# Two compression products and two heads of second attention in column halves, zero products and two DMA queues at the start

## The chip, the cores and the metric

The kernel runs on one core of one Trainium2 chip. The metric is device time in microseconds (us) of one execution, from the first instruction to the last. Engines are named as in the profile: PE (TensorE matmul), PEld (its weight loads), DVE (VectorE), ACT (ScalarE), POOL (GpSimd), SP (SyncE, which issues nearly all DMAs here).

## The reference, cut to what matters

The program is a decoder trunk of two layers over 256 tokens of width 1024, in float32. Each sub-layer is `x <- LayerNorm(alpha * x + sublayer(x))`.

- Layer 0: sliding-window attention (16 query heads, 4 key and value heads of 64), then a dense SwiGLU of inner width 3584.
- Layer 1: sparse attention (compressed, selected and window branches, each with its gate), then 8 SwiGLU experts, two for each token.

The change touches the compressed keys and values, and the last product of attention:

```
def compress(t, pos, w1, w2):
    blk = t[:, idx] + pos[None, None, :, None, :]
    flat = blk.transpose(0, 1, 3, 2, 4).reshape(B, nc, Hkv, CMP_LEN * HEAD_DIM)
    return jax.nn.gelu(flat @ w1) @ w2
kcc = compress(kc, pos_k, ck_w1, ck_w2)
vcc = compress(vc, pos_v, cv_w1, cv_w2)
...
o_s = jnp.einsum('bkgqs,bkqsd->bqkgd', p_s.astype(vsel.dtype), vsel)
```

There are 15 blocks for each of 4 key heads, laid out as 64 rows; `flat` has 2048 columns and the hidden width is 256.

## The kernel before, in words

**Tiles.** The 256 tokens are two tiles of 128 (t = 0, 1). Weights come from HBM in pieces of 1 MB into buffers called `raw` (7 of them), in the order that `plan` wrote; `load` issues them on SP as buffers come free. For the dense layers each piece is split into `hi` on ACT (L120) and `lo` on DVE (L121), in three buffers of each, and a product takes three matmuls (L204 to L206). The weights of the compression (four pieces, `w1s`) and of the experts are not split and are used as float32. Later the experts' weights also use buffers `more` and `later`, which exist once the attention's memory is given back.

**The start.** SP issues a part of the constants `cf`, both halves of the first token tile `x0`, the first two weight pieces (two DMAs each), the second token tile, and two more pieces. PE transposes x0 (L224), ACT and DVE split that into `Th` and `Tl`, and PE multiplies the first two pieces with token tile 0, then transposes x1 and does the same for tile 1. PE's order is written out by hand there; the order on ACT and DVE is a list scheduler's.

**Compression** (`compress`, L778). `X` holds keys (k = 0) and values (k = 1), laid out so that 64 of its columns are the stationary operand. For k, for each of two weight pieces q, eight matmuls of 64 columns by 256 (L803) accumulate into `hc[:, k, :]`, on PSUM partitions 0 to 63. Between k = 0 and k = 1, PE does the 16 transposes of the selected keys (`kd`, L391). A GELU follows on `hx`, 64 partitions by 512 (L807 to L815), then four transposes (L820), and two small products into `kcc` and `vcc`.

**Second attention** (`unit`, L905). For each of 8 head pairs j there are three units: (t=1, head 0), (t=1, head 1) and (t=0, both heads). A unit is a generator of four steps: scores and exponentials; division; transposes of the probabilities into `pt`; products of `pt` with values (L948) into `po`. The product of head h goes to partitions 64h to 64h + 63 of `po`. A unit of t = 1 does its four products in a row, all in one half; the unit of t = 0 alternates the halves. `attention` starts a unit each round and runs the steps of older units, the last one LAG + 1 = 4 rounds later. Tiles `p` and `pt` share eight buffers with the tag "pt".

**Experts.** For each expert, gate and up products (L1187, L1195), then down products (L1210, L1216), with weights streamed by SP.

Of the kernel before, what the change touches and what calls it, by code (L numbers as in the profile page):

```python
# [9 lines left out]
F32 = mybir.dt.float32  # L10
F32R = mybir.dt.float32r
BF16 = mybir.dt.bfloat16
# [6 lines left out]
P = 128  # L19
# [4 lines left out]
HD = 64  # L24
# [11 lines left out]
CMP_HID = 256  # L36
# [48 lines left out]
def trunk(ctx: ExitStack, tc: tile.TileContext, a, out, dbg=None):  # L85
    nc = tc.nc
    dbg = dbg or {}
    PE, ACT, DVE, POOL, SP = nc.tensor, nc.scalar, nc.vector, nc.gpsimd, nc.sync

    const = ctx.enter_context(tc.tile_pool(name="const", bufs=1))  # L90
# [6 lines left out]
    def bank(dtype=F32):  # L97
        return psum.tile([P, 512], dtype, name="ps", tag="ps")


    cbf = const.tile([P, 3 * P], BF16, name="cbf")
    cf = const.tile([P, 2 * P + 3 * NE + 9], F32, name="cf")
# [24 lines left out]
    order, raws, ready = [], [], []  # L127
# [17 lines left out]
    def plan(src, exact=True, pieces=1):  # L145
        kt, cols = src.shape[0] // P, src.shape[1]
        n = max(i for i in range(1, PART // cols + 1) if kt % i == 0)
        for k0 in range(0, kt, n):
            order.append((lambda k0=k0: src[k0 * P:(k0 + n) * P, :], n, cols, exact, pieces))
# [8 lines left out]
    def load():  # L158

        while state["loaded"] < len(order) and len(raws) < state["ahead"]:  # L160
            src, n, cols, exact, pieces = order[state["loaded"]]
            state["loaded"] += 1
            raw, kind = new_raw()
            raw = raw[:, :n * cols].rearrange("p (k f) -> p k f", k=n)
            src = src().rearrange("(k p) f -> p k f", p=P)
            pieces = min(n, pieces if state["loaded"] < len(order) - 2 else 2)
            for k in range(0, n, n // pieces):
                SP.dma_start(raw[:, k:k + n // pieces, :], src[:, k:k + n // pieces, :])
            raws.append((raw, exact, kind))
# [23 lines left out]
    def take(count=1, spare=None):  # L193

        spare = max(0, LIVE - count) if spare is None else spare
        while (raws or state["loaded"] < len(order)) and len(ready) < count + spare:
            feed()
        parts = ready[:count]
        del ready[:count]
        return parts  # L200
# [260 lines left out]
    wa, wo = a["a_w_in"][0], a["a_w_out"][0]  # L461
    plan(wa[:, :512], pieces=2)
    for c in (1024, 512):
# [19 lines left out]
    KC, VC, KS, VS, KW, VW, GL = (1024 + 256 * k for k in range(7))  # L483
    w1s = [a[w][0, q * 1024:(q + 1) * 1024, :] for w in ("b_cmp_k_w1", "b_cmp_v_w1") for q in range(2)]
    plan(wb[:, KC:KC + 512])
# [50 lines left out]
    with tc.tile_pool(name="swa", bufs=1) as pool:  # L536
# [52 lines left out]
        ps_kv, ps_q = {}, [{}, {}]  # L589
        with tc.manual_schedule(engines={PE.engine}):  # L590
            for _ in project(Ts, 512, ps_q[0], 2):
                pass
# [147 lines left out]

    zeros = const.tile([P, P], BF16, name="zeros")
    POOL.memset(zeros, 0.0)
    SP.dma_start(cmask, a["cmask"].rearrange("(t p) k c -> p t k c", p=P))
    with tc.tile_pool(name="nsa", bufs=1) as pool:
# [33 lines left out]
        def compress():  # L778
# [5 lines left out]
            DVE.tensor_copy(posT, pb[:, :32].rearrange("p (a b) -> p a b", a=2))  # L784
            hc = bank().rearrange("p (k h) -> p k h", k=2)[:C]
            Xs = wts.tile([P, 2, CMP_LEN // 2, NKV, CP], F32, name="X", tag="raw", bufs=RAW)
            for k in range(2):
# [10 lines left out]
                yield  # L798
            for k in range(2):
                for q in range(2):  # L800
                    (r,), = take()
                    for i in range(8):
                        PE.matmul(hc[:, k, :], Xs[:, k, q * 8 + i].rearrange("p g c -> p (g c)"), r[:, i, :],  # L803
                                  start=q == 0 and i == 0, stop=q == 1 and i == 7, skip_group_check=True)
                yield
            hx, hy = (pool.tile([P, 2, CMP_HID], F32, name="hx", tag="pt", bufs=PT)[:C] for _ in range(2))
            ACT.activation(hx, hc, AF.Copy)  # L807
# [8 lines left out]
            yield  # L816
            pb = bank().rearrange("p (k j c) -> p k j c", k=4, j=2)[:, :2, :, :]
            for k in range(2):
                for j in range(2):
                    PE.transpose(pb[:, k, j, :], hx[:, k, j * P:(j + 1) * P], ident[:C, :C])  # L820

# [80 lines left out]

        sums = {}

        def unit(t, j, heads):  # L905
# [36 lines left out]
            yield  # L942
            if heads[0] == 0:
                sums[t, j] = bank()[:, :P]
            po = sums[t, j]
            for m, (i, br, k) in enumerate(steps):
                h = heads[i]
                PE.matmul(po[h * HD:(h + 1) * HD, :], v[:, k, br, g, :], pt[:, m * P:(m + 1) * P],  # L948
                          start=k + br == 0, stop=False, skip_group_check=True)
            if heads[-1] == 1:  # L950
                PE.matmul(po, vcc[:, j // 4, j % 4].rearrange("p e d -> p (e d)"), pcT[:, t, j // 4, :], start=False,
                          stop=True, skip_group_check=True)
                split(oTs[t][0][:, j, :], oTs[t][1][:, j, :], po)
# [501 lines left out]
```

## Time and profile before

| | us |
|---|---|
| runs shown | 1411.89, 1413.41, 1418.05 |
| median | 1413.41 |
| the profiled execution, its own time | 1413.78 |
| its span in the trace | 1412.0 |
| PE busy | 1360.7 (96%) |
| DVE busy | 442.0 (31%) |
| ACT busy | 342.4 (24%) |

The stages by the trace: first attention to about 85 us, dense SwiGLU to about 345, second attention with its projections and the compression to about 505, the end of the layer and the router to about 545, the experts to the end. PE's busy time counts overlapping matmuls once and their ends are modelled, so a full slice may still hold slack; the time from the start of one group to the start of the next is what counts.

### The profile page before, as it was taken

The page shows a single profiled execution, that of the slowest core. Times are in us where ns is not written, and L with a number is a line of the kernel's source. Part 1 is how long each engine was busy: PE and PEld are TensorE (multiplying, and loading weights), DVE is VectorE, ACT ScalarE, POOL GpSimd, SP SyncE. Part 2 cuts the span into 40 slices and gives each one's busy share as a digit, 9 for nine tenths or more (in the row PEclk, how much of TensorE's full clock was granted, in tenths as well). Part 3 has the DMA queues.
Part 4 walks back from the last instruction along what each step waited for, and adds up shares of the span by engine and source line. Part 5 has one row for each costly group of instructions (what it writes and reads, how often), then busy time and mean ns, then how long its engine had stood idle before and what let it go on. Part 6 is the DMA issues. An engine that isn't in the chain of part 4 may idle for free. (4 is left out here: it accounts for less than half of the span.)

```text
span 1412.0 us, 23279 instructions
## 1 busy us (share of the span) xinstructions
PE 1360.7 (96%) x9761; PEld 784.5 (56%) x9762; DVE 442.0 (31%) x1004; ACT 342.4 (24%) x783; POOL 8.4 (1%) x17
## 2 busy tenths in 40 slices
PE   7999999999999999999999999999998999999984
PEld 6777888887777774453344354444343454445331
DVE  6876544556958753000101001100100100200103
ACT  5754444444456721010001001000101000100100
POOL 0000000000000000000000000000000000000000
PEclk9999999999999998999999999999999999999997
DMA  9516565554372067899999999999999999999994
GB/s 349 181 61 211 181 192 192 179 179 155 122 271 91 31 266 272 345 389 377 409 403 409 407 401 409 408 402 407 408 402 409 408 401 408 408 395 393 408 402 179
DMA packets 143679, 434.86 MB, mean 308 GB/s; under 512 B 11312, under 2 KB 18128, under 8 KB 143568
## 3 DMA queue, kind: packets, MB, share of 16 engines
q1 hardware_dynamic: 138416, 428.85, 79.3%
q10 hardware_dynamic: 5152, 4.45, 1.0%
q8 instruction: 79, 1.29, 0.4%
q14 instruction: 32, 0.26, 0.1%
HBM read 432.23 MB, written 1.05 MB: 307 GB/s over the span
## 5 line engine op out<-in xcount | busy, mean ns | idle before, releaser
L121 DVE TENSOR_TENSOR lo<-raw,hi 128x512 fp32r<-128x512 f32 (+2 forms) x244 | 166.4, 730 | 106.5 <-ACT hi L120 106.3
L1187 PE MATMUL ps<-more,Th 128*64 128x512 f32 (+1 forms) x920 | 186.8, 555 | 5.7 <-DMA more<-in_moe_w_gate 5.4
L120 ACT ACTIVATE hi<-raw 128x512 fp32r<-128x512 f32 (+2 forms) x244 | 146.0, 659 | 142.4 <-PE ps L206 129.5
L204 PE MATMUL ps<-hi,Th 128*128 128x512 f32 (+1 forms) x432 | 171.4, 397 | 4.4 <-ACT hi L120 3.2
L206 PE MATMUL ps<-hi,Tl 128*128 128x512 f32 (+1 forms) x432 | 168.6, 391 | 1.4 <-DVE Tl L121 1.4
L205 PE MATMUL ps<-lo,Th 128*128 128x512 f32 (+1 forms) x432 | 168.3, 390 | 0.0
L1244 DVE TENSOR_TENSOR h<-h,ps 128x512 f32<-128x512 f32 (+1 forms) x32 | 19.9, 621 | 448.4 <-PE ps L1187 448.4
L1187 PE MATMUL ps<-later,Th 128*64 128x512 f32 (+1 forms) x680 | 128.9, 525 | 2.1 <-DMA later<-in_moe_w_gate 1.8
L1187 PEld LDWEIGHTS ps<-more,Th 128*64 128x64 f32 x920 | 65.0, 138 | 115.5 <-issue 98.4
L204 PEld LDWEIGHTS ps<-hi,Th 128*128 128x128 f32 x432 | 81.9, 190 | 23.6 <-ACT hi L120 3.6
L1187 PE MATMUL ps<-raw,Th 128*64 128x512 f32 (+1 forms) x448 | 94.4, 561 | 0.6 <-ACT Th L1095 0.6
L1210 PE MATMUL ps<-more,hTa 128*64 128x512 f32 x408 | 92.2, 595 | 2.7 <-DMA more<-in_moe_w_down 2.7
L1236 ACT ACTIVATE h<-ps 128x512 f32<-128x512 f32 (+1 forms) x32 | 17.4, 544 | 315.1 <-PE ps L1187 315.1
L206 PEld LDWEIGHTS ps<-hi,Tl 128*128 128x128 f32 x432 | 81.8, 189 | 20.4 <-DVE Tl L121 2.9
L205 PEld LDWEIGHTS ps<-lo,Th 128*128 128x128 f32 x432 | 82.0, 190 | 16.8 <-DVE lo L121 0.4
L1187 PEld LDWEIGHTS ps<-later,Th 128*64 128x64 f32 x680 | 47.8, 137 | 72.1 <-issue 60.1
L1210 PE MATMUL ps<-later,hTa 128*64 128x512 f32 x312 | 70.3, 594 | 2.0 <-DMA later<-in_moe_w_down 2.0
L1210 PEld LDWEIGHTS ps<-more,hTa 128*64 128x64 f32 x408 | 28.4, 137 | 60.6 <-issue 54.6
L1187 PEld LDWEIGHTS ps<-raw,Th 128*64 128x64 f32 x448 | 31.7, 139 | 53.1 <-issue 48.6
L1195 PE MATMUL ps<-more,Th 128*32 128x256 f32 (+1 forms) x1136 | 60.2, 359 | 0.0
L1239 ACT ACTIVATE hb<-ps 128x256 f32<-128x256 f32 (+1 forms) x20 | 7.2, 358 | 189.0 <-PE ps L1195 189.0
L1243 DVE TENSOR_TENSOR hb<-hb,ps 128x256 f32<-128x256 f32 (+1 forms) x20 | 7.8, 388 | 142.3 <-PE ps L1195 142.3
(256 smaller groups left out, 1444.5 us busy)
## 6 DMA issues: line engine op xcount, KB each, us to landing
more<-in_moe_w_up SPq DMA_DIRECT2D x53, 1024.0 KB, 18.1
more<-in_moe_w_down SPq DMA_DIRECT2D x51, 1024.0 KB, 18.0
more<-in_moe_w_gate SPq DMA_DIRECT2D x50, 1024.0 KB, 18.2
later<-in_moe_w_down SPq DMA_DIRECT2D x38, 1024.0 KB, 15.1
later<-in_moe_w_gate SPq DMA_DIRECT2D x36, 1024.0 KB, 18.3
later<-in_moe_w_up SPq DMA_DIRECT2D x35, 1024.0 KB, 18.0
raw<-in_moe_w_gate SPq DMA_DIRECT2D x26, 1024.0 KB, 18.0
raw<-in_moe_w_up SPq DMA_DIRECT2D x24, 1024.0 KB, 18.2
```

The source lines that it names most:

```text
L120: state["act"] = ACT.activation(hi, src, AF.Copy)
L121: DVE.tensor_tensor(lo, src, hi.bitcast(F32), op=OP.subtract)
L204: PE.matmul(ps, xh, wh, start=first, stop=False)
L205: PE.matmul(ps, xh, wl, start=False, stop=False)
L206: PE.matmul(ps, xl, wh, start=False, stop=last)
L1187: PE.matmul(pa[h * CA:(h + 1) * CA, :wide // 2], T[:, k, :CA], parts[k // n][:, k % n, h * wide // 2:(h + 1) * wide // 2], start=k == 0, s ...
L1195: PE.matmul(pb[q * CB:(q + 1) * CB, :wide // 4].rearrange("p (b f) -> p b f", f=CB), T[:, k, CA:], w[:, q], start=k == 0, stop=k == KT - 1)
L1210: PE.matmul(ya[o * CA:(o + 1) * CA, :], hT[0][:, f % (n // 2), f // (n // 2), :], parts[f // 2][:, f % 2, o * 512:(o + 1) * 512], **ends(f))
L1236: ACT.activation(ha, ga[:, :wide // 2], AF.Silu)
L1239: ACT.activation(hb, gb[:, :wide // 4], AF.Silu)
L1243: DVE.tensor_tensor(hb, hb, ub[:, :wide // 4], op=OP.mult)
L1244: DVE.tensor_tensor(ha, ha, ua[:, :wide // 2], op=OP.mult)
```

## The change

- **Start.** `zeros` is made on DVE at the beginning instead of on POOL later. PE multiplies zeros 7 times before the transposes of x0 and 5 times behind them, into a bank that nobody reads. The first weight piece is issued on ACT's queue, and the first two pieces come in four DMAs each instead of two.
- **Compression.** The pieces are planned as (key q, value q) for q = 0, 1. The key product goes to partitions 0 to 63 and the value product to 64 to 127 of one 256-wide region, in turn. The GELU then works on 128 by 256, and two full transposes take the place of four.
- **Second attention.** The products of (t=1, head 0) are not issued with their unit, but kept and issued with those of head 1, sorted so that the two halves take turns.

```
+    zeros = const.tile([P, P], BF16, name="zeros")
+    DVE.memset(zeros, 0.0)
...
-                SP.dma_start(raw[:, k:k + n // pieces, :], src[:, k:k + n // pieces, :])
+            queue = ACT if len(order) > 99 and state["loaded"] == 1 else SP
+                queue.dma_start(raw[:, k:k + n // pieces, :], src[:, k:k + n // pieces, :])
...
-    plan(wa[:, :512], pieces=2)
+    plan(wa[:, :512], pieces=4)
...
-    w1s = [a[w][0, q * 1024:(q + 1) * 1024, :] for w in ("b_cmp_k_w1", "b_cmp_v_w1") for q in range(2)]
+    w1s = [a[w][0, q * 1024:(q + 1) * 1024, :] for q in range(2) for w in ("b_cmp_k_w1", "b_cmp_v_w1")]
...
+            idle = bank()
+            def turn_over(n):
+                for _ in range(n):
+                    PE.matmul(idle, zeros, zeros.unsqueeze(1).to_broadcast([P, 4, P]), start=True, stop=True)
+            turn_over(7)
+            Ts[0]
+            turn_over(5)
             for _ in project(Ts, 512, ps_q[0], 2):
...
-            hc = bank().rearrange("p (k h) -> p k h", k=2)[:C]
+            hc = bank()[:, :CMP_HID]
...
-            for k in range(2):
-                for q in range(2):
-                    (r,), = take()
-                    for i in range(8):
-                        PE.matmul(hc[:, k, :], Xs[:, k, q * 8 + i].rearrange("p g c -> p (g c)"), r[:, i, :],
-                                  start=q == 0 and i == 0, stop=q == 1 and i == 7, skip_group_check=True)
+            for q in range(2):
+                r = [w for (w,) in take(2, 1 + q)]
+                for i in range(8):
+                    for k in range(2):
+                        PE.matmul(hc[k * C:(k + 1) * C, :], Xs[:, k, q * 8 + i].rearrange("p g c -> p (g c)"),
+                                  r[k][:, i, :], start=q == 0 and i == 0, stop=q == 1 and i == 7,
+                                  skip_group_check=True)
                 yield
-            hx, hy = (pool.tile([P, 2, CMP_HID], F32, name="hx", tag="pt", bufs=PT)[:C] for _ in range(2))
+            hx, hy = (pool.tile([P, CMP_HID], F32, name="hx", tag="pt", bufs=PT) for _ in range(2))
...
-            if heads[0] == 0:
+            if heads[-1] == 1:
                 sums[t, j] = bank()[:, :P]
-            po = sums[t, j]
-            for m, (i, br, k) in enumerate(steps):
-                h = heads[i]
-                PE.matmul(po[h * HD:(h + 1) * HD, :], v[:, k, br, g, :], pt[:, m * P:(m + 1) * P],
-                          start=k + br == 0, stop=False, skip_group_check=True)
+            po = sums.get((t, j))
+            held = waiting.setdefault((t, j), [])
+            held += [(k, br, heads[i], pt, m) for m, (i, br, k) in enumerate(steps)]
             if heads[-1] == 1:
+                for k, br, h, x, m in sorted(held, key=lambda e: e[:3]):
+                    PE.matmul(po[h * HD:(h + 1) * HD, :], v[:, k, br, g, :], x[:, m * P:(m + 1) * P],
+                              start=k + br == 0, stop=False, skip_group_check=True)
```

**Order on ACT at the start.** The names are buffers: `Th` is the upper part of a transposed token tile (first x0, then x1), `hi` that of a weight piece. Before:

```order
L120 ACT_TABLE_LOAD
L120 ACTIVATE Th_112<-ps_114 128x512
L120 ACTIVATE Th_112<-ps_121 128x512
L120 ACTIVATE hi_128<-raw_84 128x512 x4
L120 ACTIVATE hi_140<-raw_87 128x512 x4
L120 ACTIVATE Th_188<-ps_190 128x512
L120 ACTIVATE Th_188<-ps_197 128x512
L120 ACTIVATE hi_152<-raw_91 128x512 x4
```

The third weight piece (`raw_91` here, `raw_97` below) stands behind `Th` of x1. After:

```order
L172 DMA raw_86<-in_a_w_in 128x512 x4
L122 ACT_TABLE_LOAD
L122 ACTIVATE hi_147<-raw_86 128x512
L122 ACTIVATE Th_124<-ps_126 128x512
L122 ACTIVATE Th_124<-ps_133 128x512
L122 ACTIVATE hi_147<-raw_86 128x512 x3
L122 ACTIVATE hi_159<-raw_91 128x512 x4
L122 ACTIVATE hi_171<-raw_97 128x512 x4
L122 ACTIVATE Th_207<-ps_209 128x512
L122 ACTIVATE Th_207<-ps_216 128x512
```

The four copies of the third piece have moved ahead of `Th` of x1; DVE's order moved in the same way.

**Order on PE behind that.** What PE does with x1 (`Th_207`) once it is transposed, in the change; before, all 24 products of tile 1 stood in a row here:

```order
L208 MATMUL ps_146<-hi_147,Th_207 128x512
L209 MATMUL ps_146<-lo_148,Th_207 128x512
L208 MATMUL ps_248<-hi_171,Th_124 128x512
L209 MATMUL ps_248<-lo_172,Th_124 128x512
L210 MATMUL ps_248<-hi_171,Tl_125 128x512
L210 MATMUL ps_146<-hi_147,Tl_208 128x512
```

Three products of the third piece with tile 0 have moved ahead of the first product that needs `Tl` of x1.

**Order on ACT behind the compression.** `kd` are copies of rotated keys for which PE waits there, `hi_3615` and `hi_3566` the upper parts of the weight pieces that follow. Before:

```order
L120 ACTIVATE hi_3473<-raw_3350 128x512 x4
L852 ACTIVATE v_2937<-ps_3381 128x24
L120 ACTIVATE hi_3551<-raw_3370 128x512 x4
L857 ACTIVATE v_2937<-ps_3471 128x232
L120 ACTIVATE hi_3615<-raw_3382 128x512 x4
L120 ACTIVATE kd_3495<-rot_3489 128x512
```

After:

```order
L122 ACTIVATE hi_3490<-raw_3367 128x512 x4
L864 ACTIVATE v_2954<-ps_3398 128x24
L122 ACTIVATE hi_3566<-raw_3379 128x512 x4
L122 ACTIVATE kd_3512<-rot_3506 128x512
L869 ACTIVATE v_2954<-ps_3488 128x232
```

Three groups of copies stood ahead of `kd`, now two do; the four copies of the third piece stand behind it.

**Order on PE in second attention.** `pt_3885` and `pt_3915` are the transposed probabilities of heads 0 and 1 of one pair at t = 1. Before, the two heads stood apart:

```order
L948 MATMUL ps_3911<-pt_3870,v_2937 64x128 x4
L391 MATMUL ps_3916<-cf_71,qs_3823 128x128 x4
L391 MATMUL ps_3922<-cf_71,qs_3823 128x128 x4
L939 MATMUL ps_3941<-cf_71,p_3838 128x128 x4
L917 LDWEIGHTS cbf_70
L917 MATMUL ps_3950<-masks_75,cbf_70 128x512
L920 MATMUL ps_3950<-kT_2936,qT0_2938 128x256 x4
L948 MATMUL ps_3911<-pt_3900,v_2937 64x128 x4
L951 MATMUL ps_3911<-pcT_2943,vcc_2941 128x128
```

After:

```order
L963 MATMUL ps_3971<-pt_3885,v_2954 64x128
L963 MATMUL ps_3971<-pt_3915,v_2954 64x128
L963 MATMUL ps_3971<-pt_3885,v_2954 64x128
L963 MATMUL ps_3971<-pt_3915,v_2954 64x128
L963 MATMUL ps_3971<-pt_3885,v_2954 64x128
L963 MATMUL ps_3971<-pt_3915,v_2954 64x128
L963 MATMUL ps_3971<-pt_3885,v_2954 64x128
L963 MATMUL ps_3971<-pt_3915,v_2954 64x128
L965 MATMUL ps_3971<-pcT_2960,vcc_2958 128x128
```

All eight stand at head 1's place and take turns; the six rows that stood between the two groups (transposes, the mask, scores of the next unit) now stand ahead of both.

## Rows read from the trace of the kernel before

**Rows 1.** Busy time by stretch: second attention, then experts; columns in the first line.

```profile
core 0: us, PE busy (x) PEld busy (x) DVE busy (x) ACT busy (x) POOL busy (x), PEclk, DMA share, GB/s
424.30:507.00 82.70, 81.94 (x562) 65.52 (x561) 63.13 (x209) 55.17 (x195) 0.00 (x0) 1.00 0.19 65
560.00:570.00 10.00, 10.00 (x98) 4.15 (x94) 0.00 (x0) 0.87 (x2) 0.00 (x0) 1.00 0.46 148
1100.00:1200.00 100.00, 100.00 (x966) 46.79 (x966) 7.13 (x16) 6.30 (x14) 0.00 (x0) 1.00 1.03 406
```

**Rows 2.** Timeline of the start: start us, us, engine, line, operation, tiles, idle before.

```profile
2.15 2.00 SPq L168 DMA_DIRECT2D raw<-in_a_w_in  x4
4.24 1.94 PE L224 MATMUL ps<-cf,x 128*128 128x128 f32 x8 [4.24 <-DMA x<-in_x]
9.39 0.79 PE L204 MATMUL ps<-hi,Th 128*128 128x512 f32 x1 [3.21 <-ACT hi L120]
13.27 0.63 PE L206 MATMUL ps<-hi,Tl 128*128 128x512 f32 x1
13.70 0.63 PE L204 MATMUL ps<-hi,Th 128*128 128x512 f32 x1
18.75 0.50 PE L204 MATMUL ps<-hi,Th 128*128 128x512 f32 x1 [0.25 <-ACT Th L120]
19.07 2.19 ACT L120 ACTIVATE hi<-raw 128x512 fp32r<-128x512 f32 x4
19.81 0.39 PE L204 MATMUL ps<-hi,Th 128*128 128x512 f32 x1
20.05 0.39 PE L205 MATMUL ps<-lo,Th 128*128 128x512 f32 x1
```

**Rows 3.** DMA at the start: two stretches, then one issue (KB, us to landing).

```profile
2.00:6.00 4.00, 1.76 (x8) 1.44 (x8) 0.01 (x1) 0.66 (x2) 0.00 (x0) 1.00 0.77 255
7.00:16.00 9.00, 6.61 (x18) 4.98 (x19) 5.71 (x9) 4.60 (x8) 0.00 (x0) 1.00 1.04 395
raw<-in_a_w_in SPq DMA_DIRECT2D x1, 1024.0 KB, 11.7
```

**Rows 4.** Timeline of PE: the halves of the compression; a gate product of an expert.

```profile
389.86 7.12 PE L803 MATMUL ps<-raw,X 128*64 128x256 f32 x32
396.91 1.97 PE L391 MATMUL ps<-cf,kd 128*128 128x128 f32 x16
398.81 7.12 PE L803 MATMUL ps<-raw,X 128*64 128x256 f32 x32
602.30 7.09 PE L1187 MATMUL ps<-more,Th 128*64 128x512 f32 x32
```

**Rows 5.** Behind the compression: timelines of ACT and PE.

```profile
419.11 2.19 ACT L120 ACTIVATE hi<-raw 128x512 fp32r<-128x512 f32 x4 [1.18 <-PE ps L206]
421.87 0.65 PE L391 MATMUL ps<-cf,kd 128*128 128x128 f32 x4 [2.80 <-ACT kd L120]
```

**Rows 6.** Timeline of PE in second attention.

```profile
450.57 1.09 PE L948 MATMUL ps<-pt,v 128*64 128x128 f32 x8 [0.76 <-ACT pt L941]
453.74 1.09 PE L948 MATMUL ps<-pt,v 128*64 128x128 f32 x8
454.75 0.49 PE L951 MATMUL ps<-pcT,vcc 128*128 128x128 f32 x2
456.20 0.66 PE L948 MATMUL ps<-pt,v 128*64 128x128 f32 x8
456.79 0.49 PE L951 MATMUL ps<-pcT,vcc 128*128 128x128 f32 x2
```

**Rows 7.** A wait of PE near the end, and the granted clock behind it; another stretch.

```profile
1368.87 5.36 PE L1187 MATMUL ps<-more,Th 128*64 128x256 f32 x32 [3.35 <-DMA more<-in_moe_w_gate]
1369.30:1372.80 3.50, 3.50 (x22) 1.89 (x18) 0.00 (x0) 0.00 (x0) 0.00 (x0) 0.51 1.05 389
530.00:540.00 10.00, 9.42 (x28) 4.88 (x30) 6.21 (x35) 3.30 (x5) 0.00 (x0) 0.50 0.47 138
```

More of the change, by code (lines that the diff above doesn't have):

```diff
@@ L738, in trunk @@
     keep("x2", xs)
-    zeros = const.tile([P, P], BF16, name="zeros")
-    POOL.memset(zeros, 0.0)
     SP.dma_start(cmask, a["cmask"].rearrange("(t p) k c -> p t k c", p=P))
@@ L816, in compress @@
             yield
[L817 to L820, printed above, removed]
+            pb = bank()[:, :CMP_HID].rearrange("p (j k c) -> p k j c", j=2, k=2)
+            for j in range(2):
+                PE.transpose(pb[:, :, j, :].rearrange("p k c -> p (k c)"), hx[:, j * P:(j + 1) * P], ident)
             hk = pool.tile([P, 2, C], F32, name="hk", tag="pt", bufs=PT)
@@ L901, in compressed @@
             ACT.activation(pcT[:, :, u, :], pb, AF.Copy)
-        sums = {}
+        sums, waiting = {}, {}
         def unit(t, j, heads):
```

## The prediction

> **What bounds the kernel now.** I read the page first: PE is busy for 1360.7 of the span's 1412.0 us, DVE and ACT for under a third (the table above). So time can only be won where PE's own work shrinks or where PE waits, and I took the three places of the change one after the other: busy time by stretch, then PE's timeline there, then the clock. In second attention PE is busy for 81.94 of 82.70 us, DVE for 63.13, ACT for 55.17 [rows 1]: PE sets the pace, the other two have 20 to 27 us of slack. Its timeline has one wait of 0.76 us, for ACT's `pt` [rows 6]. In the compression PE runs through two blocks of 32 records in 7.05 us each (389.86 to 396.91, and the second alike), 1.97 us of transposes between them [rows 4]. Behind it PE waits 2.80 us for `kd` [rows 5]. At the start PE waits 4.24 us for x0 and 3.21 us for `hi`, and then its products stand 0.43 us apart (13.27 to 13.70) [rows 2], nearly twice the 0.24 us of later ones (19.81 to 20.05): the lower of PE's two levels (1.2 and 2.4 GHz), though the granted clock reads 1.00 there [rows 3].
>
> An earlier end of attention must also survive the experts, where the DMA share is 1.03. Just ahead of that, at 560 to 570, it is 0.46 while PE is full [rows 1]: transfers wait for buffers there, so an earlier PE frees buffers earlier and the whole train of transfers moves up with it. I carry savings over one to one.
>
> The profiled execution took 1413.78, 0.4 above the median of 1413.41; the sum is made against 1413.78.
>
> **Compression.** The two products of 64 columns go to the two column halves in turn. The bounds for such a pair: no overlap (0 saved) and full overlap (half). The nearest row is an expert's gate product, also 64 columns and also alternating halves: 32 records of 512 columns in 7.09 us [rows 4], as long as 32 records of 256 columns in one half. So two halves run beside each other at full rate, and 64 records of 256 columns should take 7.05 in place of 14.1: **-7.05**. The GELU on 128 by 256 halves what DVE does per partition and two transposes go; PE's next projection covers both, so I count nothing for them. The wait of 2.80: `kd` stood behind three groups of copies, the last at 419.11 for 2.19 us after 1.18 us of waiting for PE [rows 5]; with that group moved behind `kd`, 2.19 + 1.18 = 3.37 us go from the path, more than the wait: **-2.80**. What is late next is the moved group of weight copies, for which PE has transposes to do first. The 1.97 us of transposes stay; were they, no longer between two blocks, to leave PE waiting for the second pair of pieces, 1.97 would be lost. Together -9.85, bounds -5.1 (7.05 - 1.97, and the wait stays) to -9.85. The order of the pieces (key, value, key, value) moves two loads past each other on SP; both are issued well ahead, so nothing.
>
> **Second attention.** Head 0's group of 8 records takes 453.74 to 454.75 = 1.01 us in one half; the alternating group of t = 0 takes 456.20 to 456.79 = 0.59 [rows 6]. In one half a record costs 1.01 / 8 = 0.126, so in turn half of that, and eight more records add 0.50. Sixteen in turn then cost 0.59 + 0.50 = 1.09 in place of 2.02: 0.93 us for each of 8 pairs, -7.4 at most. Against it: PE has less to do in each round, while ACT's copy to `pt` stays. The seen wait for it is 0.76 [rows 6]. If every pair has that wait, 8 x 0.76 = 6.1 goes back and 1.3 is left. I take a third of it, 0.25 a pair, since ACT has 27 us of slack and only one such wait is there now: **-5.4**, bounds -1.3 to -7.4.
>
> **Start.** `zeros` on DVE and 12 zero products: DVE and PE have nothing before x0, and the cover of the products is the waits of 4.24 and 3.21 [rows 2]; without cover, 12 x 0.43 = 5.2 us. ACT's four issues: SP took 2.00 us for four [rows 2], beside the same 4.24. If the zeros keep PE at its upper speed, tile 0's 24 products take 24 x 0.24 = 5.8 us. But tile 1 now stands behind the copies of the third piece on ACT. That piece was issued at 5.01 and landed 11.7 later, at 16.7 [rows 3]. From 7 to 16 the DMA share is 1.04, so only the idle part of 2 to 6 can bring it forward: 4 x (1 - 0.77) = 0.92, to 15.8. Four copies take 2.19 [rows 2] and one of `Th` a quarter of that, 0.55: tile 1 begins at 18.5 against 18.75. Its first three products took 1.06 (18.75 to 19.81 [rows 2]), waiting for `Tl`; with three other products put ahead they take 3 x 0.24 = 0.72. That gains 0.25 + 0.34 = 0.6. PE, however, is done with tile 0 at 9.39 - 0.92 + 5.8 = 14.3 with the transposes of x1 (half of x0's 1.94 [rows 2] at the upper level) at 15.3, and idles for 3.2. A wait of 3.35 was followed by 3.4 us of clock 0.51, half of the upper speed [rows 7]; one of 2.80 [rows 5] by none. 3.2 is nearer the former, so I take 3.4 / 2 = 1.7 of loss: **+1.1**. Bounds: no fall, -0.6; the long fall (10 us at 0.50 [rows 7], 5.0 lost) and a third piece no earlier, +5.3.
>
> Does the second queue bring anything forward? The rows show only the idle part of 0.92 us. The Trainium skill (DMA: Bandwidth & Descriptors, section Issuing engines are not separate DMA queues) says that DMAs of different engines end up on the same 16 DMA engines and that issuing from several saves only issue time. By it the third piece would land at 16.7 as before, the start would cost 2.0, and the total would be 1400.5.
>
> **Sum.** 1413.78 - 9.85 - 5.4 + 1.1 = **1399.6**, 1.0% below the profiled execution.
>
> **Rivals.**
> 1. *The start pays and attention in full*: no clock fall (-0.6) and -7.4. For it: the idle of 3.2 may as well be like the 2.80 that did no harm. Against: two terms must both be at their ends. 1413.78 - 9.85 - 7.4 - 0.6 = 1395.9. Chance 0.20.
> 2. *ACT becomes attention's bound*: every pair waits 0.76 for `pt`, and only 1.3 is won: 1403.7. For it: the wait exists already. Against: ACT is busy for only 55 of 82.7 us. The Trainium skill (TensorEngine Tiling (Array Packing), section PSUM Bottleneck) warns that tiling speeds up TensorE but not the copies out of PSUM, which may become the bottleneck; by that rule this rival is the likeliest, and the trace bears it out only by that one wait. Chance 0.15.
> 3. *The long clock fall at the start*: 5.0 in place of 1.7: 1402.9. Chance 0.08.
> 4. *The halves don't overlap*, in either place, since two stationary operands of 64 columns with 256 or 128 moving ones switch too fast. Only the 2.80 is won and 1.1 lost: 1412.1. Against it: the 0.59 of the alternating group. Chance 0.07.
> 5. *Slower: buffers run out.* `p` and `pt` share eight buffers. Head 0's `pt` is now held until head 1's products; by my count of the steps seven are then live, and two of a query rotation would make nine. A stalled unit costs up to its round, 82.7 / 24 = 3.45 us; one for each of 8 pairs costs 27.6: 1427.2. It decides as soon as live tiles exceed eight in every pair. Against it: rotations are not in every pair. Chance 0.05.
>
> **How the numbers follow.** My own case has the remaining 0.45. About 0.5%, 7 us, can be told from no change, so the bound for faster is 1406.3. Rivals 1 to 3 and my case lie below it, 0.88 in all; 0.03 of this I move to no change, for small losses that add up. Faster 0.85, same 0.10, slower 0.05. The range reaches past rival 1 for unknown sizes of the same sign and past rivals 2 and 3 together (1407.0): 1391 to 1408; what is left out is rivals 4 and 5 and some tails, under 0.2.
>
> **What would show it.** Right: one block of 64 records for about 7 us in place of two; no 2.8 us wait for `kd`; groups of 16 records in turn of about 1.0 us; tile 0's first products 0.24 apart; PE waiting some 3.2 us for `Th` of x1 with a clock of about 0.5 behind it. Wrong: `pt` waits of 0.7 us or more in most pairs (rival 2), 16 records in 2 us (rival 4), waits for a buffer on ACT ahead of `pt` (rival 5), or an experts' stage that begins 15 us earlier and yet ends where it did.

## The result and the profile after

| | before | after |
|---|---|---|
| median of the runs | 1413.95 (1411.89 to 1418.05) | 1393.17 (1389.74 to 1394.49) |
| the profiled execution, its own time | 1413.78 | 1389.74 |
| its span | 1412.0 | 1387.9 |

The ratio is 0.9846 (95% interval 0.9817 to 0.9874): 1.5% faster, some 20.8 us between the medians, where 14.2 had been forecast. The two profiled executions lie 24.0 us apart; the one of after was the fastest of its four runs, so the pair shows some 3 us more than the medians.

The page of after, its span and the busy time of the engines:

```profile
span 1387.9 us, 23321 instructions
PE 1345.9 (97%) x9771; PEld 773.8 (56%) x9772; DVE 439.6 (32%) x1005; ACT 342.2 (25%) x783; POOL 8.2 (1%) x16
```

PE's share went from 96% to 97%: work left PE, and waits went with it. Six points that both traces have divide the gain. Each number is the start of PE's row at that point.

| point on PE | before | after | earlier by | gained in this stretch |
|---|---|---|---|---|
| first record of the compression | 389.86 | 387.28 | 2.58 | 2.58 |
| first product behind its second block | 405.86 | 396.38 | 9.48 | 6.90 |
| `kd` transposes behind it | 421.87 | 409.02 | 12.85 | 3.37 |
| last product with `vcc` (end of second attention) | 506.33 | 484.53 | 21.80 | 8.95 |
| first product with `pick` (router) | 525.61 | 504.28 | 21.33 | -0.47 |
| last down product of the experts | 1392.29 | 1367.93 | 24.36 | 3.03 |

The -0.47 ahead of the router comes with the change of attention: this stretch takes 19.73 to 19.75 us in every profile that has it, and 19.28 or 19.29 in every other. Of the 24.36 us at the last point, 24.27 are there at the first down product already (580.69 before, 556.42 after).

**The start**, timeline of after; the rows that answer to [rows 2]:

```profile
1.03 3.17 PE L599 MATMUL ps<-zeros 128*128 128x512 bf16 x7 [1.03 <-DVE zeros L102]
5.26 2.32 PE L228 MATMUL ps<-cf,x 128*128 128x128 f32 x8 [1.06 <-DMA x<-in_x]
9.49 0.39 PE L209 MATMUL ps<-lo,Th 128*128 128x512 f32 x1
9.72 0.39 PE L210 MATMUL ps<-hi,Tl 128*128 128x512 f32 x1
14.23 2.19 ACT L122 ACTIVATE hi<-raw 128x512 fp32r<-128x512 f32 x4 [2.37 <-DMA raw<-in_a_w_in]
16.32 1.06 ACT L122 ACTIVATE Th<-ps 128x512 fp32r<-128x512 f32 x2
16.95 0.50 PE L208 MATMUL ps<-hi,Th 128*128 128x512 f32 x1 [1.09 <-ACT Th L122]
```

PE multiplies zeros from 1.03 on. The transposes of x0 come a microsecond later than before (5.26; x0 now shares the transfers with the first weight piece), but tile 0's products stand 0.23 us apart from the second on (9.49 to 9.72), where it was 0.43 or more up to the eleventh (14.13). ACT has the third piece at 14.23, and tile 1 begins at 16.95 after a wait of 1.09 us. The DMA issue of that piece and the stretch from 2 to 6 us, for [rows 3]:

```profile
raw<-in_a_w_in SPq DMA_DIRECT2D x1, 1024.0 KB, 7.8
2.00:6.00 4.00, 2.94 (x10) 1.19 (x8) 0.69 (x1) 1.91 (x2) 0.00 (x0) 1.00 0.96 330
```

It was issued 1.43 us later than before (about 6.44 against 5.01) and landed 7.8 us on instead of 11.7, so by 14.2 in place of 16.7. The share in 2 to 6 is 0.96, it was 0.77.

**The compression**, PE's timeline of after, for [rows 4, 5]:

```profile
387.28 3.67 PE L815 MATMUL ps<-raw,X 128*64 128x256 f32 x32
390.88 1.97 PE L395 MATMUL ps<-cf,kd 128*128 128x128 f32 x16
392.78 3.67 PE L815 MATMUL ps<-raw,X 128*64 128x256 f32 x32
396.38 0.40 PE L208 MATMUL ps<-hi,Th 128*128 128x280 f32 x1
409.02 0.66 PE L395 MATMUL ps<-cf,kd 128*128 128x128 f32 x4
```

Two blocks of 3.60 us replace two of 7.05; the 1.90 us of transposes between them remain. The last row has no wait in brackets: the 2.80 us for `kd` are gone. ACT's timeline shows why:

```profile
406.25 2.19 ACT L122 ACTIVATE hi<-raw 128x512 fp32r<-128x512 f32 x4 [1.05 <-issue]
408.35 0.61 ACT L122 ACTIVATE kd<-rot 128x512 fp32r<-128x512 f32 x1
```

Only the group of copies at 406.25 stands right ahead of `kd`, and `kd` is copied from 408.35 on, just in time for PE. The group that used to wait 1.18 us for PE and then take 2.19 [rows 5] now follows later. The stretch of 3.37 in the table is the wait of 2.80 and 0.57 in PE's rows ahead of it. Those hold two transposes of the GELU in place of four (0.13 us in place of 0.39), and 94 products in place of 96: two of 0.13 us each now stand behind the first of `kd`'s transposes.

**Second attention**, PE's timeline of after, for [rows 6]:

```profile
431.19 1.09 PE L963 MATMUL ps<-pt,v 128*64 128x128 f32 x16
432.21 0.49 PE L965 MATMUL ps<-pcT,vcc 128*128 128x128 f32 x2
433.64 0.66 PE L963 MATMUL ps<-pt,v 128*64 128x128 f32 x8
437.83 0.30 PE L951 MATMUL ps<-cf,p 128*128 128x128 f32 x1 [0.75 <-DVE p L946]
```

Sixteen records in turn take 1.02 us (431.19 to 432.21; in one of the eight pairs 1.34), and t = 0's eight still 0.59. No row of this stage waits for `pt` any more; two wait for DVE's `p`, 0.23 and 0.75 us.

**Behind the router**, one row of PE and one stretch (PE's clock is the number behind the last bracket, 1.00 for the upper level and 0.50 for the lower), for [rows 7]:

```profile
508.45 1.13 PE L1106 MATMUL ps<-pick,x 128*128 128x96 f32 x8 [0.54 <-DVE pick L1089]
510.00:515.00 5.00, 4.84 (x16) 2.55 (x18) 2.92 (x18) 2.45 (x5) 0.00 (x0) 0.66 0.61 210
```

The eight records at 508.45 take 1.13 us where those of before, at 529.78, took 2.02 at the lower clock. The stretch of lower clock is some 3.4 us long here and was 10.2. No term of the prediction had that.

### The profile page after: what moved, and what is told of

Same layout as the page of the kernel before. It is cut to its first block, busy times and chain, and to the rows that moved or that the text cites. A ratio compares the mean times of both kernels' runs of the same rounds, so it can differ in the third digit from the quotient of the medians.

```text
span 1387.9 us, 23321 instructions
## 1 busy us (share of the span) xinstructions
PE 1345.9 (97%) x9771; PEld 773.8 (56%) x9772; DVE 439.6 (32%) x1005; ACT 342.2 (25%) x783; POOL 8.2 (1%) x16
```

## The experiments

All twelve runs do the whole work of the reference. Times are medians in us, ratios are to the kernel before on the same chip, with the 95% interval; "best" is the fastest execution. Three chips were used: e1 to e4 ran on one (before's median there was 1412.98), e5 to e8 on a second (1413.01), e9 to e12 on a third (1417.68). So times and ratios of runs from different chips can be compared only roughly. The last two columns are the length of PE's lower clock (about 0.50) in the one profiled execution of each, behind the `kd` wait and behind the router, summed over windows of 1 us.

| run | median (executions) | best | ratio | kd wait | router |
|---|---|---|---|---|---|
| before, profiled | 1413.78 | | | none | 10.2 |
| e1 start alone | 1411.95 (12) | 1410.96 | 0.9993 (0.9975 to 1.001) | 3.4 | 10.2 |
| e8 zero products alone | 1411.60 (12) | 1409.75 | 0.9979 (0.9963 to 0.9996) | 3.4 | 13.7 |
| e2 compression alone | 1402.36 (6) | 1396.77 | 0.9904 (0.988 to 0.9928) | none | 6.8 |
| e3 attention alone | 1401.99 (6) | 1400.66 | 0.9916 (0.9893 to 0.994) | 3.4 | none |
| e4 attention, head by head | 1405.99 (11) | 1403.10 | 0.9944 (0.9924 to 0.9963) | 13.7 | 3.4 |
| e5 before, router filled | 1411.86 (12) | 1406.81 | 0.9981 (0.9963 to 1.0) | none | none |
| e6 as e4, router filled | 1407.66 (7) | 1402.55 | 0.9941 (0.9917 to 0.9964) | 3.4 | none |
| e10 as e3, router filled | 1399.56 (6) | 1399.03 | 0.9892 (0.9866 to 0.9917) | 3.4 | none |
| the change, profiled | 1389.74 | | | none | 3.4 |
| the change again (e9) | 1391.70 (6) | 1387.37 | 0.9828 (0.98 to 0.9857) | none | 6.8 |
| e7 the change, router filled | 1387.79 (5) | 1387.40 | 0.9811 (0.9787 to 0.9835) | none | none |
| e11 as e7, end filled | 1387.65 (5) | 1386.14 | 0.9798 (0.9774 to 0.9822) | none | 3.4 |
| e12 as e11, start filled | 1387.41 (5) | 1385.89 | 0.9801 (0.9776 to 0.9827) | none | none |

### The parts alone

**e1.** Only the start; compression and attention as before:

```
-    plan(wa[:, :512], pieces=2)
+    plan(wa[:, :512], pieces=4)
...
+            queue = ACT if len(order) > 99 and state["loaded"] == 1 else SP
...
+            turn_over(7)
+            Ts[0]
+            turn_over(5)
```

> Only the start of the change (zero products, first piece on ACT's queue, four DMAs for each of the first two pieces). My theory after seeing the changed profile: the compression begins 2.6 us earlier than before (at about 387.3 us) since the third piece lands near 14 us, tile 1 begins near 17 us and PE does not fall to the lower clock; everything behind is shifted by that alone, so about -2.6 us. Rival: the start alone costs time (+1.1 us, as the prediction had it), and what the full change shows there comes from elsewhere. A further rival: the shorter low-clock stretch behind the router (10.2 us before, about 3.5 us in the change) comes with the start; then another -2.5 us.

Measured: no difference that can be told (-0.07%, interval -0.25 to +0.1%); the medians differ by 1.0. The compression begins at 387.18, 2.7 us ahead of the before profile. But six other runs with the start of before begin it at 387.70 to 389.21 (e4, e2, e6, e3, e5, e10): the profile of before was a late one, because the first weights landed late in it (ACT's first `hi` at 8.71; it was 7.08 in e4 and 7.10 in e2). In the seven profiles with the new start or its zeros it begins at 387.18 to 388.48. The means of the two groups, seven profiles each, are 388.8 and 387.9, so the start is worth about 1 us, not 2.6, and not a loss. The clock behind the router fell for 10.2 us as before: that gain does not come with the start.

**e8.** Of the start only the zeros, `turn_over(7)` and `turn_over(5)`:

```
+    DVE.memset(zeros, 0.0)
...
+            turn_over(7)
+            Ts[0]
+            turn_over(5)
             for _ in project(Ts, 512, ps_q[0], 2):
```

> Only the 12 zero products at the start, no second queue and two DMAs a piece as before. Theory: tile 0's products stand 0.24 apart instead of 0.43, but DVE's lo (0.67 each for three products) sets the pace, and x1's transposes begin about 2 us earlier than the 17.47 of before; the compression begins at 386 to 388 us. If the second queue is what counts, no gain. In total -1 to -2.5 us.

Measured: -0.21% (interval -0.37 to -0.04%), 1.4 us by the medians. Tile 1 begins where it does in the full change (16.95):

```profile
16.91 0.51 PE L206 MATMUL ps<-hi,Th 128*128 128x512 f32 x1 [0.25 <-ACT Th L122]
```

The zeros alone bring it there, and the compression begins at 387.44. The second queue and the four DMAs add nothing on top that these runs can tell, though with them the third piece landed at 14.1 (e1) and not at 16.8 (e8).

**e2.** Only the compression, from `w1s` to the two transposes as in the diff above:

```
-            hc = bank().rearrange("p (k h) -> p k h", k=2)[:C]
+            hc = bank()[:, :CMP_HID]
...
+            for q in range(2):
+                r = [w for (w,) in take(2, 1 + q)]
+                for i in range(8):
+                    for k in range(2):
```

> Only the compression of the change. My theory: 64 records of 256 columns in two column halves take 7.1 to 7.3 us in two blocks of about 3.6 (14.1 before), and the wait of 2.80 us for kd goes, in all -9.5 to -10.3 us by the end of the second block of kd transposes. Rival: the wait for kd only goes because the start shifts the order on ACT; then -7 us and the wait stays.

Measured: 0.9904, 10.6 us by the medians. PE's timeline at the first block, behind the second, and at the `kd` transposes:

```profile
388.12 3.67 PE L803 MATMUL ps<-raw,X 128*64 128x256 f32 x32
393.62 3.67 PE L803 MATMUL ps<-raw,X 128*64 128x256 f32 x32
409.85 0.65 PE L391 MATMUL ps<-cf,kd 128*128 128x128 f32 x4
```

The blocks and the transposes between them take 9.10 us (388.12 to the next product at 397.22; 16.00 before), and `kd` comes 12.63 us behind (16.01 before) with no wait. So the new order on ACT belongs to the compression, not to the start; the rival falls. By the trace 6.90 + 3.38 = 10.3 us. That the wait went because a group of copies moved behind `kd` is read from the order and the times of ACT's rows; no run changes this order alone.

**e3.** Only second attention:

```
+                for k, br, h, x, m in sorted(held, key=lambda e: e[:3]):
+                    PE.matmul(po[h * HD:(h + 1) * HD, :], v[:, k, br, g, :], x[:, m * P:(m + 1) * P],
```

> Only second attention of the change (head 0's products held and put in turn with head 1's). My theory: each of 8 pairs takes 1.0 us less with no new wait of more than 1 us in all, -8 to -9 us between the first kd transposes behind the compression and the last vcc product. Rival (my own term): waits for pt give back part and -5.4 is left.

Measured: 0.9916, 11.0 us by the medians. From the `kd` transposes to the last `vcc` product PE takes 76.84 us, 7.6 less than before, although the clock fell there for 3.4 us in this execution. There are no `pt` waits. Without such a fall the stretch takes 75.5 us in all five profiles of the change, with fillings or without, and 84.4 to 84.5 in those of before, e2 and e5: attention's part is 8.9 us, less the 0.47 ahead of the router. The rest of the 11.0 is not attention's: in this profile the clock did not fall at all behind the router.

### Taking turns, or standing together?

**e4.** The held products are issued at head 1's place, but head by head:

```
-                for k, br, h, x, m in sorted(held, key=lambda e: e[:3]):
+                for k, br, h, x, m in held:
```

> As the run with second attention alone, but the held products are issued head by head (four of head 0, then four of head 1) at the place of head 1. If the gain comes from the two halves taking turns, sixteen records take 2.0 us and the time is that of the kernel before within 1 us. If it comes from the place (a later product group waits less for pt), a part of the 8 us stays; the wait of 0.76 us alone should go.

Measured: 0.9944, 7.0 us faster. My expectation failed: sixteen records do not take 2.0 us. In e6, the same order (its clock was undisturbed from 426 on), PE's timeline reads

```profile
444.33 1.58 PE L951 MATMUL ps<-pt,v 128*64 128x128 f32 x16
445.84 0.49 PE L953 MATMUL ps<-pcT,vcc 128*128 128x128 f32 x2
```

that is 1.51 us for sixteen, against 1.03 in turn (e3):

```profile
444.42 1.09 PE L951 MATMUL ps<-pt,v 128*64 128x128 f32 x16
445.45 0.38 PE L953 MATMUL ps<-pcT,vcc 128*128 128x128 f32 x1
```

Half of the gain comes from the two groups standing together. Eight records in one half take 1.02; eight of the other half directly behind them add only 0.49, so the two halves run beside each other where the groups meet: the second group's first record starts at 444.82, while three of the first group's eight are still to start. Taking turns saves the other 0.48. By eight pairs: 4.2 and 3.8.

In e4's own profile the stretch of attention shows nothing of this (84.84 us against 84.46 before), and the reason is the clock. PE's wait for `kd`, and the clock behind it:

```profile
419.72 0.66 PE L391 MATMUL ps<-cf,kd 128*128 128x128 f32 x4 [2.80 <-ACT kd L120]
422.00:434.00 12.00, 12.00 (x46) 10.51 (x46) 7.75 (x20) 2.21 (x6) 0.00 (x0) 0.50 0.53 176
```

The prediction had taken this wait of 2.80 us as harmless, since the profile of before shows no fall behind it. Of the eight profiles that still have the wait, six show a fall there: 3.4 us in five, 13.7 in this one. None of the six profiles with the new compression, which removes the wait, has it.

A second such place lies in first attention, and the new start made it. Before, PE's two longest waits there, both for DVE's `p`, are 0.87 us at 53.59 and 1.40 at 56.97; in all six profiles with the whole new start one wait of 2.07 or 2.08 us stands in their place. In three of the six (e9, e11, e12) the clock falls there for 3.4 us; e12's row and the stretch behind it:

```profile
54.95 0.45 PE L581 MATMUL ps<-cf,p 128*128 128x128 f32 x1 [2.07 <-DVE p L575]
55.00:56.00 1.00, 1.00 (x6) 0.94 (x7) 1.00 (x5) 0.50 (x2) 0.00 (x0) 0.50 0.00 0
```

e9 and e12 also have a fall of 3.4 us from 7 on, among the zeros and tile 0's first products, and e7 has one at 18. In these four profiles the compression begins at 388.21 to 388.48; in the three without a fall ahead of it (the change's first, e1, e8), at 387.18 to 387.44.

### The clock behind the router

**e5.** Twelve products of zeros in PE's waits there; they add zero to banks that are being summed:

```
+            def fill(ps, n):
+                for _ in range(n):
+                    PE.matmul(ps.rearrange("p (k s) -> p k s", k=4), zeros, identb.unsqueeze(1).to_broadcast([P, 4, P]),
+                              start=False, stop=False, skip_group_check=True)
...
+                    fill(banks[0], 3)
...
+                    fill(banks[0], 3)
...
+                            fill(banks[1], 6)
```

> The kernel before, with 12 products of zeros added to PE's waits behind the router (3, 3 and 6, into banks that take them as plus zero). Theory: the clock of 0.50 behind the router, 10.2 us long in the profile of before, is the price of those waits; filled, it goes or shortens to under 3 us and the time falls by 3 to 5 us. Rival: the fall has its cause before these waits, or the products only delay the gate product by what they take (12 x 0.22 = 2.6 us, less the waits of some 2.3); then no gain.

```profile
527.58 0.81 PE L1087 MATMUL ps<-cbf,zeros 128*128 128x512 bf16 x3
528.31 0.81 PE L1087 MATMUL ps<-cbf,zeros 128*128 128x512 bf16 x3
530.00 1.46 PE L1087 MATMUL ps<-cbf,zeros 128*128 128x512 bf16 x6
532.26 1.08 PE L1199 MATMUL ps<-raw,Th 128*64 128x512 f32 x4
524.00:540.00 16.00, 15.80 (x108) 8.94 (x112) 12.39 (x64) 4.50 (x7) 0.93 (x1) 1.00 0.50 193
```

The clock stays at 1.00, and from the last `vcc` product to the first down product PE needs 69.34 us where it needed 74.36: 5.0 less, half of 10.2. All fourteen profiles bear that price out. From the first `pick` product to the first down product PE takes 50.1 us in the five that are filled and have no fall, 50.6 in e3, 51.5 to 52.2 with a fall of 3.4 us, 53.3 with 6.8, 55.1 with 10.2 and 55.8 with 13.7. Yet the median gains only 1.2 (0.9981, interval 0.9963 to 1.0), which is hardly told from nothing. The fastest executions, 1406.81 and 1407.28 at a mean clock of 0.995, lie some 6 us below the median of before; the slower ones, up to 1416.72, have means of 0.985 to 0.988. Where their clock fell isn't known: one execution of each kernel is profiled.

**e6.** e4 with the same filling.

> The attention change issued head by head (as in the fourth run), with the same 12 products of zeros. If that run's 7 us came from the clock behind the router, this one stands within 1.5 us of the kernel before with the same filling. If they came from attention itself, it stays 5 to 7 us below it.

Measured: 4.2 below e5 by the medians, 4.3 by the fastest executions, so neither of the two expectations. The sixteen records alone show as much (8 x 0.53 = 4.2). But in e6's profile the clock fell for 3.4 us inside attention, and in e5's it did not (the stretch took 80.0 and 84.5 us), so the two are not alike but for the order; that some 2.7 of e4's 7.0 us came with the clock is an estimate.

**e10.** e3 with the same filling.

> Second attention of the change alone, heads in turn, with the 12 products of zeros behind the router. Theory: beside the kernel before with the same filling it gains 7.6 us (16 records in 1.03 instead of 2 x 1.02, eight pairs), of which the run head by head with filling already had 4.4; so 1403 to 1405 us. Rival: the 11 us of the run without filling are all attention's; then 1401 us.

Measured: by the fastest executions 7.8 below e5, which ran on another chip (1399.03 and 1406.81), by the medians 12.3. The first is near attention's part, as the trace has it (76.27 us from `kd` to the last `vcc` product, 84.47 in e5). That the medians lie further apart goes with the clock: e5's middle executions ran at a mean of 0.988, e10's at 0.993 and 0.994. Why the kernels with the new attention fall less often is open.

**e7.** The change with the same filling.

> The changed kernel with the same 12 products of zeros. Its fall behind the router was only some 3.5 us in the profile: theory, a gain of 1 to 2 us at most; rival (the products cost their own time), 0 to 1 us slower.

Measured: 1387.79, a ratio of 0.9811; the change itself had 0.9846 and, in e9, 0.9828 on other chips. The intervals overlap, and e9's fastest execution (1387.37) is as fast as this kernel's (1387.40): that the filling pays is likely, not shown by the times. The median fell by more than expected; a likely part of it is that the change's fall behind the router can be longer than the 3.4 us of its first profile (6.8 in e9). At the start of this execution the clock fell, behind a wait of 1.86 us for `Th` of x1:

```profile
18.00:22.00 4.00, 4.00 (x12) 3.22 (x12) 1.52 (x4) 0.00 (x0) 0.00 (x0) 0.58 1.06 382
```

That is the fall which the prediction had counted there, and the compression then began at 388.46 instead of 387.28.

**e9.** The change again, unaltered.

> The changed kernel again, unaltered, on the chip of the next three runs: 1390 to 1395 us. Theory: its profile shows other lengths of the lower clock behind the router and near the end than the first one (3.4 and 6.8 us there), while the stretches between fixed points of PE's work (compression 9.2 us, second attention 75.5 us) repeat within 0.1 us.

Measured: 1391.70. The compression takes 9.10 us and attention 75.51, both as in the first profile; the clock behind the router falls for 6.8 us. The first down product comes 2.31 us later than in the first profile (558.73 and 556.42), and the last block of sixteen 2.67 later; first the row of the first profile, where a wait of 0.17 us splits the sixteen into 12 and 4, then e9's:

```profile
1364.97 2.79 PE L1224 MATMUL ps<-raw,hTa 128*64 128x512 f32 x12 [0.53 <-ACT hTa L1267]
1367.64 4.00 PE L1224 MATMUL ps<-raw,hTa 128*64 128x512 f32 x16 [0.53 <-ACT hTa L1267]
```

So a delay ahead of the experts arrives at the end in full.

### The end, and a kernel with all fillings

PE's timeline of the change where the last weights arrive: a wait of 3.36 us and behind it 32 records at the lower clock:

```profile
1344.57 6.55 PE L1201 MATMUL ps<-more,Th 128*64 128x256 f32 x32 [3.36 <-DMA more<-in_moe_w_gate]
1357.74 1.94 PE L1224 MATMUL ps<-later,hTa 128*64 128x512 f32 x8 [0.53 <-DMA later<-in_moe_w_down]
```

**e11** and **e12.** e7, and in both

```
+                if len(jobs) > 1 and job == len(jobs) - 1 and c == len(WIDE) - 1:
+                    for _ in range(14):
+                        PE.matmul(ga, zeros, zeros.unsqueeze(1).to_broadcast([P, 4, P]), start=True, stop=True)
                 gate_up(ga, gb, x.T, wide)
```

and in e12 `Ts[1]` and `turn_over(4)` behind tile 0's products at the start.

> The changed kernel with the 12 products behind the router and 14 more zero products ahead of the last gate product, where PE waits 3.36 us for its weights and runs at 0.50 to 0.65 behind it for 6.8 us in the profile of the change. Theory: the lower clock goes, but the waits for weights behind it (0.53 and 0.74 us in that profile) grow by what PE gains, so less than 1 us beside the changed kernel with the 12 alone. Rival: PE sets the end, and 1.7 to 3.4 us are won.

> As the run before, with 4 zero products more behind the transposes of x1 at the start, where PE waits 1.09 us for Th. Theory: in some executions (one of three profiles of the changed start) the clock falls there for 3.4 us; filled, that goes, and the median falls by 0 to 0.6 us. Rival: the four products delay tile 1 by what they overrun, up to 0.9 us.

Measured: 1387.65 and 1387.41, beside 1387.79 of e7 on another chip: no difference that can be told. (e9, on their own chip, has 1391.70, but it lacks the filling behind the router too.) e12's timeline at the end:

```profile
1340.15 3.20 PE L1262 MATMUL ps<-zeros 128*128 128x512 bf16 x14
1346.30 1.95 PE L1215 MATMUL ps<-more,Th 128*64 128x256 f32 x16 [0.76 <-DMA more<-in_moe_w_gate]
1351.70 1.95 PE L1215 MATMUL ps<-later,Th 128*64 128x256 f32 x16 [0.76 <-DMA later<-in_moe_w_up]
1354.35 1.94 PE L1238 MATMUL ps<-later,hTa 128*64 128x512 f32 x8 [0.70 <-DMA later<-in_moe_w_down]
1343.00:1360.00 17.00, 13.12 (x90) 5.95 (x90) 0.42 (x1) 0.98 (x2) 0.00 (x0) 1.00 1.04 401
```

The clock is 1.00 in this stretch and nothing is won: most blocks of 16 or 8 records now wait for weights (0.76, 0.76, 0.70), at a DMA share of 1.04. e7 and e9 alone would not settle this, as their clock does not fall near the end without the filling either. But from the first to the last down product all fourteen profiles take 811.99 to 812.40 us: before (a fall of 3.4 us near the end) 812.09, the change (6.8) 811.99, e9 (none) 812.31. Transfers set the length of this stage, and a PE at half speed only took up waiting. At the start the four products ended about when `Th` came: tile 1 begins at 17.13, 16.95 in the change, and the compression at 388.32, with the two falls at 7 and 55 ahead of it.

## Why the prediction was right, and where it was not

The range (1391 to 1408) holds 1393.17, and faster was right. The likeliest case, 1399.6, was 6.4 too slow. Attention, the start and the router's clock all missed to the same side, so that the range held by only 2.2 us; the profiled execution, 1389.74, lies outside it. By terms, with what the profiled pair shows:

| term | predicted | measured |
|---|---|---|
| compression and the wait behind it | -9.85 | -10.27 (6.90 + 3.37) |
| second attention | -5.4 | -8.95 |
| start | +1.1 | -2.58 in this pair, -0.9 by the means of seven profiles each |
| router's clock | none | -3.03 in this pair |

- **Compression: right.** Two halves in turn run at full rate, and with the group of copies behind `kd` the wait of 2.80 went. I had counted nothing for the two transposes that go; they are about half of the 0.57 beyond the wait, and the two products that moved behind `kd` are the other half. 64 records took 7.20 us, where 7.05 had been taken over from an expert's gate product.
- **Second attention: the step that failed is "If every pair has that wait ... I take a third of it, 0.25 a pair".** No pair waits for `pt`. With head 0's products a unit later there is more time for ACT's copy, and the one wait of 0.76 went as well. The products themselves won 7.8 (seven pairs 1.02, one 0.70), the wait 0.76, and two new waits for `p` cost 0.98, which makes 7.6 of the 8.95. The other 1.3 lies in the rows beside the groups and isn't fully placed: the record ahead of each group stands 0.20 to 0.22 us ahead of it, where score products of the same shape mostly stand 0.12 apart, and there are eight groups fewer. Sixteen records took 1.02 and not the 1.09 that I had worked out. By the Trainium skill (TensorEngine Tiling (Array Packing), section PSUM Bottleneck) the copies out of PSUM could have become the limit; this trace does not bear it out (waits for `pt`: 0.76 us before, none after).
- **Start: the step that failed is "only the idle part of 2 to 6 can bring it forward".** I left the landing of the third piece at its old delay of 11.7 less 0.92; it was 7.8, the DMA share from 7 to 16 being full in both. With the piece at 14.2 PE waited 1.09 and not 3.2, and the clock did not fall in this execution, though in e7 it did, for 3.4 us behind a wait of 1.86. I had also left out first attention, where the new start makes a wait of 2.07 us, with a fall of the clock behind it in three of six profiles. What the profile of before could not tell is that its own first weights came late.
- **Second queue: right that it buys little.** e8 has tile 1 at 16.91 without it. The Trainium skill (DMA: Bandwidth & Descriptors, section Issuing engines are not separate DMA queues) says that issuing from several engines saves only issue time; the times agree (e1 is not faster than e8), while the third piece did land 2.5 us earlier with queue and smaller pieces. No run separates these two.
- **The clock: missing as a term.** The sum took the falls of before as given. They vary: behind the router between none and 13.7 us in kernels whose instructions there are the same. In this pair that was worth 3 us. For the start, the lower level was read from products 0.43 us apart while the clock read 1.00 [rows 2, 3]; the profile of before has its first record of the clock only at 14.3 us, where the products come to stand 0.23 apart, so the 1.00 ahead of that says nothing.
- **One to one: right.** What PE had won at the first down product, 24.27 us, was 24.36 at the last, and e9's delay of 2.31 there was 2.67 at the last block. The stage between takes 812 us in every profile; only what PE wins inside it (e11, e12) is lost, since transfers set its length.
- **Rivals.** Rival 1 is nearest: start and attention in full, 1395.9, still 2.7 above the result. Rivals 2 (no `pt` wait in the trace), 4 (1.02 for sixteen records) and 5 (PE waits less than 1 us in the whole stage) are refuted; rival 3 needs a long fall at the start, and the falls there were of 3.4 us each.

## What to carry to other kernels

Put products for different column halves directly behind each other, best in turn: here even whole groups, one behind the other, gave half of the gain. Look at what a step that you move stands behind in its engine's queue, since a copy for which PE waits may cost more than the work you save, and may also cost clock behind the wait (here in six of eight profiles). Before you charge or credit a term of a microsecond or two from one profile, ask whether its landing times and clock falls would be the same in the next execution; fill PE's short waits with products that add nothing, and see whether transfers then set the end. Compare the same record in two profiles, not the starts of merged rows, which can be split differently.

## What was not expected of the hardware

- Eight records in one column half take 1.02 us alone, and eight of the other half directly behind them add 0.49, without taking turns (e6).
- The granted clock behind the same instructions differs from execution to execution: behind a wait of 2.80 us none, 3.4 or 13.7 us at half, behind one of 2.07 us none or 3.4, behind the router's waits of some 0.5 us none to 13.7. Twelve products of zeros kept it at 1.00 there in the profiles of e5, e6, e7, e10 and e12, but not in e11 (3.4 us).
- With the start of before, the same instructions in each of seven kernels, ACT began on the first weights between 7.08 and 8.71 us.
- From the first to the last down product 14 profiles of 13 kernels agree within 0.41 us in 812, with falls of the clock of none to 6.8 us inside.
